# The norm between retention and the second MLP, with its multiplies divided among three engines

## The chip, the cores and the metric

The kernel runs on one core of one Trainium2 chip. The metric is device time in microseconds from the first to the last instruction with what lies around them; the time of a kernel is the median of several runs. The engines are named here as in the profile: PE is TensorE (PEld its weight loads), DVE is VectorE, ACT is ScalarE, POOL is GpSimd, SP issues DMAs.

## The reference

A decoder trunk of two layers works on 1024 positions of 1024 channels in float32. Layer 0 mixes by dilated attention and a short convolution, layer 1 by retention; after each mixer come an RMS norm and a gated MLP with a depthwise convolution of width 3. Only the last of these norms is touched:

```python
def rms_norm(x, g):
    xf = x.astype(jnp.float32)
    y = xf * lax.rsqrt(jnp.mean(xf * xf, axis=-1, keepdims=True) + EPS)
    return (y * g.astype(jnp.float32)).astype(x.dtype)

def conv_glu_ffn(xn, w_up, conv_w, w_down):
    u = causal_dwconv(xn @ w_up, conv_w)
    g, val = jnp.split(u, 2, axis=-1)
    return (jax.nn.silu(g) * val) @ w_down

        x = x + retention_mixer(...)
        x = x + conv_glu_ffn(rms_norm(x, ffn_norm[l]), ffn_w_up[l], ffn_conv_w[l], ffn_w_down[l])
```

## The kernel before

The residual stream stays on the chip as eight row tiles of 128 positions by 1024 channels (`xb`). Float32 products are made from a high and a low half of each operand: `split` (lines 107 to 110) casts the source on ScalarE (line 109, the high half) and subtracts it on GpSimd or VectorE (line 110, the low half); each product then takes three passes of TensorE (high by high, high by low, low by high).

The up-projections use one level of Strassen's scheme. Row tiles are taken in pairs, (0, 2), (1, 3), (4, 6) and (5, 7), one tile from each of the two row halves of the scheme's blocks. For each pair the class `Norming` (line 720) does four things, and a plan, a string of steps, says in which order the program writes them down:

- `q`: the sum of squares on ScalarE (line 163; its unused output goes to a scratch tile of the tag "s", of which there are three), then the inverse rms on GpSimd (lines 152 and 153);
- `r`: the normed rows. In the form that this norm has, VectorE multiplies each tile by the inverse rms and the norm weights in two instructions of 512 channels (`normed`, line 172);
- `t`: 16 transposes on TensorE (`turn`, line 179) into four PSUM banks of the tag "b", which has four;
- `c`: from the four transposed blocks, the seven operands of the scheme, split into halves (`xc`). `combine` (line 184) copies one block on ScalarE, makes four sums on VectorE (lines 196, 198, 199, 201) that all go to SBUF, and splits seven operands: three blocks straight from PSUM with their low halves on VectorE, the four sums with their low halves on GpSimd.

The class knows a second form, `spread=True`, which the norm ahead of the first MLP uses. A step `g` multiplies both tiles of the pair by the norm weights on GpSimd (`gain`, line 735), four instructions of 512 channels a pair. The step `r` then multiplies one tile by its inverse rms on ScalarE (line 764) and the other on VectorE (line 762), in place, in one instruction of 1024 channels each. And `c` is `combine_psum` (line 206): four sums again, but two of them are written over blocks in PSUM, so that VectorE makes five low halves and GpSimd two:

```python
        act.copy(b12, p12)
        put(0, p11)
        dve.tensor_tensor(t3, p22, b12, ALU.subtract)
        put(5, t3, pool)
        dve.tensor_tensor(t2, t3, p11, ALU.add)
        put(4, t2, pool)
        dve.tensor_tensor(p11, b12, p11, ALU.subtract)
        put(2, p22)
        put(1, p21)
        put(3, p11)
        dve.tensor_tensor(p21, t2, p21, ALU.subtract)
        put(6, p21)
```

Two other strands of work run through the plan. `d` is one step of the last output sweep of retention: 12 matmuls for one row tile (line 328) and two adds to `xb` (line 333). The sweep has eight steps, four for each of two groups of rows of the output weights, over the tiles 4, 6, 5, 7, so tiles 0 to 3 are complete before it starts and tiles 4 to 7 only near its end. `h` is one step of the first block of the up-projection (`first_block`, then `strassen`, line 231): one step that loads weights and forms sums of them (lines 274 to 276, scratch tiles of the tag "s" as well), then 14 products (line 245), seven on the columns of pairs 1 and 2 and seven on those of pairs 3 and 4. Each weight operand is split when its product is near; the low halves of the weight sums are instructions of VectorE (line 110, `hl<-s`).

Row tiles, the temporary tiles of `c`, the block's outputs and two of the four operands of the last sweep share five buffers of the tag "u". Before the plan starts, `play("q0 r0 q1")` (line 1357) is written down behind the last unit of retention. The plan is `PLAN_LATE` (line 35), played at line 1367. The program's order is not the exact order of an engine's queue: when the kernel is built, a planner lays each engine's instructions out by its own costs, and where several are ready takes the one written down first. On the chip each queue then runs in that fixed order.

Of the kernel before, what the change touches and what calls it, by code (L numbers as in the profile page):

```python
# [31 lines left out]
FILL = (1, 2)  # L32

PLAN = "s0 g0 q0 s1 q1 r0 t0 s2 q2 c0 g1 r1 s3 q3 t1 c1 g2 h1 r2 t2 h1 c2 g3 r3 h1 t3 h1 c3 h4"
PLAN_LATE = "d1 t0 d1 c0 r1 d1 t1 d1 c1 d2 q2 h1 r2 d1 t2 d1 q3 h1 c2 r3 h1 t3 h1 c3 h4"

PLAN_DOWN = (
    "a0 d2 a1 d2 a2 d2 a3 d2 A0 d3 b0 b1 B0 A1 B1",
# [36 lines left out]
def trunk(tc, a):  # L75
# [79 lines left out]
    def row_gains(g, parts):  # L155

        for i, t in enumerate(parts):
            sync.dma_start(out=t, in_=g[0:1, i * HALF : (i + 1) * HALF].to_broadcast([P, HALF]))
        return parts
# [178 lines left out]
    def run(gen):  # L338
        for _ in gen:
            pass  # L340
# [14 lines left out]
    g0 = row_gains(a["even_norm"][0:1], [np_.tile([P, HALF], f"g{i}") for i in range(2)])  # L355
    load_x(1)
    r0 = np_.tile([P, P], "r0")
# [295 lines left out]
    def fill(n):  # L653
        for _ in range(n):
            next(steps, None)
# [129 lines left out]
    nrm = Norming(a["ffn_norm"][0:1], spread=True)  # L785
# [377 lines left out]
    def fetch_q(h, half):  # L1163
        q = rt[0].tile([P, 2, 2, HALF], "q", 2, dt=F32R)
        sync.dma_start(out=f(q), in_=qscr[4 * h + 2 * half])
        return q

    def fetch_k(h, half):

        k, kf = rt[1].tile([P, 2, 2, HALF], "k", dt=F32R), None  # L1170
        sync.dma_start(out=f(k), in_=qscr[4 * h + 2 * half + 1])
        if half == 0:
            kf = rt[1].tile([P, 2, HALF], "kf")
            sync.dma_start(out=kf, in_=kscr[h])
        return k, kf
# [3 lines left out]
    def scores(q, k):  # L1179
        sT = rt[3].tile([P, 2, 1280], "sT", dt=F32R)  # L1180
        for j in range(4):
            n = HALF - j * P
            b = b_bank()
            for d in range(2):
                for i, (ks, qs) in enumerate(PASSES):
                    pe.matmul(
                        b[:, :n], k[:, ks, d, j * P : (j + 1) * P], q[:, qs, d, j * P :],
                        start=(d == 0 and i == 0), stop=(d == 1 and i == 2),
                    )
            t = wk.tile([P, HALF], "s", 3)  # L1190
            dve.tensor_tensor(t[:, :n], b[:, :n], unit0["tri"][:, :n], ALU.mult)
            split(sT[:, 0, SOFF[j] : SOFF[j] + n], sT[:, 1, SOFF[j] : SOFF[j] + n], t[:, :n], (pool, dve)[j % 2])
        return sT

    def key_rows(kf):

        kn = rt[3].tile([P, 4, HALF], "ky", dt=F32R).rearrange("p t (s d) -> p t s d", s=2)
        for t in range(4):
            pt = b_bank()
            for d in range(2):  # L1200
                pe.transpose(pt[:, d * P : (d + 1) * P], kf[:, d, t * P : (t + 1) * P], ident)
            act.copy(kn[:, t, 0, :], pt[:, :256])
            dve.tensor_tensor(kn[:, t, 1, :], pt[:, :256], f(kn[:, t, 0, :]), ALU.subtract)
        return kn

    def first_state(kn, v):

        pd = [o_bank(), o_bank()]
        for t in range(4):
            for d in range(2):  # L1210
                for i, (ks, vs) in enumerate(PASSES):
                    pe.matmul(
                        pd[d], kn[:, t, ks, d * P : (d + 1) * P], v[:, vs, t, :],
                        start=(t == 0 and i == 0), stop=(t == 3 and i == 2),
                    )
        st = rt[3].tile([P, 2, 2, HALF], "st", dt=F32R)
        for d in range(2):
            act.copy(st[:, 0, d, :], pd[d])
            dve.tensor_tensor(st[:, 1, d, :], pd[d], f(st[:, 0, d, :]), ALU.subtract)
        return st  # L1220

    def outputs(half, q, v, sT, st):
        y = f(rt[3].tile([P, 4, HALF], "ky", dt=F32R))
        held = []

        def scale(t, o, mv, r):
            dve.tensor_scalar(y[:, t, :], o, mv[:, 0:1], r, ALU.subtract, ALU.mult)

        for t in range(4):
            o = b_bank()  # L1230
            terms = [(sT[:, :, SOFF[j] + (t - j) * P : SOFF[j] + (t - j + 1) * P], v[:, :, j, :]) for j in range(t + 1)]
            if half:
                terms += [(q[:, :, d, t * P : (t + 1) * P], st[:, :, d, :]) for d in range(2)]
            for n, (l, r) in enumerate(terms):
                for i, (ls, rs) in enumerate(PASSES):
                    pe.matmul(
                        o, l[:, ls, :], r[:, rs, :], start=(n == 0 and i == 0), stop=(n == len(terms) - 1 and i == 2)
                    )
            bs, mv, r = rt[3].tile([P, 6], "bs", 3), rt[3].tile([P, 2], "mv", 3), sm.tile([P, 1], "rr", 8)
            dve.bn_stats(bs, o)  # L1240
            dve.bn_aggr(mv, bs)
            rsqrt_mean(r, mv[:, 1:2], 1, 1)
            held.append((t, o, mv, r))
            fill(OFILL[half][t])
            if t:
                scale(*held.pop(0))
        return y, lambda: scale(*held.pop(0))

    def gated(h, y, gt, last):
        if last:  # L1250
            t = h_tile()
            yT = [t[:, :, i * HALF : (i + 1) * HALF] for i in range(2)]
            yT += [u_tile().bitcast(F32R).rearrange("p (s t) -> p s t", s=2) for _ in range(2)]
        else:
            t = [yp.tile([P, 2, 2, HALF], f"y{i}", dt=F32R) for i in range(2)]
            yT = [t[c // 2][:, :, c % 2] for c in range(4)]
        for c in range(4):
            pt = b_bank()
            for t in range(4):
                pe.transpose(pt[:, t * P : (t + 1) * P], y[:, t, c * P : (c + 1) * P], ident)  # L1260
            dve.scalar_tensor_tensor(gt[:, c, :], pt, gncol(h, c), gt[:, c, :], ALU.mult, ALU.mult)
            split(yT[c][:, 0], yT[c][:, 1], gt[:, c, :], (pool, dve)[c % 2])
        return yT

    def wo_sweep(half, h, yT, g, tiles, after=None):
        def lhs(j):
            return lambda s, t: yT[2 * g + j][:, s, (t - 4 * half) * P : (t - 4 * half + 1) * P]

        return sweep(
            [lhs(j) for j in range(2)], [w_rows(wo, h * 4 + 2 * g + j) for j in range(2)], tiles, o_bank, after  # L1270
        )

    def fetch_v(h, half, queue=act):
        v = rt[4 if half else 2].tile([P, 2, 4, HALF], "v", dt=F32R)
        for s in range(2):
            queue.dma_start(out=f(v[:, s]), in_=vscr[2 * h + half, :, s])
        return v

    def fetch_g(h, half):
        t, ts = rt[3].tile([P, 4, HALF], "gt"), slice(half * HALF, (half + 1) * HALF)  # L1280
        sync.dma_start(out=t, in_=scr[4 * h : 4 * h + 4, :, ts].rearrange("a p t -> p a t"))
        return t
# [26 lines left out]
    for h in range(4):  # L1309
        for n, block in enumerate(blocks[h]):  # L1310
# [4 lines left out]
            c0 = (h * (4 if name == "ret_wg" else 2) + i) * P  # L1315
# [17 lines left out]
    for n, (h, half) in enumerate(units):  # L1333
        more = n + 1 < len(units)
        sT = scores(q, k)
        fill(SFILL[half][0])
        if half == 0:
            kn = key_rows(kf)
            fill(SFILL[half][1])
            st = first_state(kn, v)  # L1340
        if more:
            q2, (k, kf) = fetch_q(*units[n + 1]), fetch_k(*units[n + 1])
        y, finish = outputs(half, q, v, sT, st)
        if more:
            q = q2
            fill(SFILL[half][2])
            v = fetch_v(*units[n + 1])
        finish()
        if more:
            run(steps)  # L1350
        else:
            fill(2)
        yT = gated(h, y, gt, not more)
        if not more:
            run(steps)
            nrm = Norming(a["ffn_norm"][1:2])
            nrm.play("q0 r0 q1")
        if more:
            gt = fetch_g(*units[n + 1])
            tiles = range(4 * half, 4 * half + 4)  # L1360
            steps = chain(*[wo_sweep(half, h, yT, g, tiles) for g in range(2)])
# [4 lines left out]
    head = first_block(a["ffn_w_up"][1], 0, NFF * P, xc)  # L1366
    nrm.play(PLAN_LATE, xc, chain(*[wo_sweep(half, h, yT, g, ORDER[4:]) for g in range(2)]), head[0])

# [50 lines left out]
```

## Time and profile before

| | |
|---|---|
| three runs | 2714.38, 2716.61, 2719.99 us; median 2716.61 us |
| the profiled execution | 2716.35 us, of which its span 2714.6 us |
| granted TensorE clock, mean | 0.995 of full speed |
| HBM read, written | 257.38 MB, 77.07 MB |
| DMA, mean rate | 124 GB/s |

Every time in the views counts from the start of the span of the profiled execution. An engine is busy while an instruction of it runs; TensorE's matmuls overlap, so that a mean duration is longer than the distance from one to the next, and that distance is the better price. A name such as `u<-xb,rr,g` gives the tile written and the tiles read. The idle time in brackets is that of the engine just before the instruction, with the one that ended it.

### The profile page before, as it was taken

The page shows a single profiled execution, that of the slowest core. Times are in us where ns is not written, and L with a number is a line of the kernel's source. Part 1 is how long each engine was busy: PE and PEld are TensorE (multiplying, and loading weights), DVE is VectorE, ACT ScalarE, POOL GpSimd, SP SyncE. Part 2 cuts the span into 40 slices and gives each one's busy share as a digit, 9 for nine tenths or more (in the row PEclk, how much of TensorE's full clock was granted, in tenths as well). Part 3 has the DMA queues.
Part 4 walks back from the last instruction along what each step waited for, and adds up shares of the span by engine and source line. Part 5 has one row for each costly group of instructions (what it writes and reads, how often), then busy time and mean ns, then how long its engine had stood idle before and what let it go on. Part 6 is the DMA issues. An engine that isn't in the chain of part 4 may idle for free. (4 is left out here: it accounts for less than half of the span.)

```text
span 2714.6 us, 34985 instructions
## 1 busy us (share of the span) xinstructions
PE 2643.7 (97%) x12793; PEld 2167.6 (80%) x12793; DVE 1907.7 (70%) x2950; ACT 1189.6 (44%) x2050; POOL 795.3 (29%) x603
## 2 busy tenths in 40 slices
PE   8999999999999999989999999999999999999999
PEld 6877777778888888867979888788877888888887
DVE  4247776687777789697575665566578777777986
ACT  4345543454444444364444444222235444445444
POOL 6721113533343300033222122344454433331000
PEclk9999999999999999999999999999999999999999
DMA  5310012122222274424545556655421222225554
GB/s 173 104 47 28 24 36 78 40 75 90 74 85 79 78 271 151 159 84 143 187 163 167 185 166 244 243 191 194 155 70 56 82 82 78 85 71 194 201 185 143
DMA packets 258784, 336.74 MB, mean 124 GB/s; under 512 B 15120, under 2 KB 182196, under 8 KB 252468
## 3 DMA queue, kind: packets, MB, share of 16 engines
q1 hardware_dynamic: 224428, 246.94, 28.2%
q10 hardware_dynamic: 34184, 87.57, 8.8%
q8 instruction: 100, 1.64, 0.2%
q14 instruction: 72, 0.59, 0.1%
HBM read 257.38 MB, written 77.07 MB: 123 GB/s over the span
## 5 line engine op out<-in xcount | busy, mean ns | idle before, releaser
L110 POOL TENSOR_TENSOR hl<-raw,hl 128x512 fp32r<-128x512 f32 x347 | 580.4, 1687 | 1243.0 <-ACT hl L109 1121.5
L245 PE MATMUL b<-xc,hl 128*128 128x512 f32 (+1 forms) x2652 | 606.7, 389 | 4.7 <-POOL xc L110 3.0
L245 PE MATMUL o<-xc,hl 128*128 128x512 f32 (+1 forms) x2568 | 592.4, 391 | 14.1 <-ACT u L300 5.2
L245 PEld LDWEIGHTS b<-xc,hl 128*128 128x128 f32 x2652 | 488.1, 190 | 117.3 <-POOL xc L110 3.8
L245 PEld LDWEIGHTS o<-xc,hl 128*128 128x128 f32 x2568 | 474.9, 191 | 125.6 <-ACT u L300 7.6
L109 ACT CAST hl<-raw 128x512 fp32r<-128x512 f32 (+1 forms) x440 | 265.2, 609 | 515.0 <-PE o L328 136.8
L110 DVE TENSOR_TENSOR hl<-s,hl 128x512 fp32r<-128x512 f32 x309 | 219.3, 714 | 228.7 <-ACT hl L109 228.5
L972 DVE SCALAR_TENSOR_TENSOR u<-u,cc,u 128x1022 f32<-128x1022 f32 (+1 forms) x176 | 263.5, 1522 | 0.9
L109 ACT CAST hl<-s 128x512 fp32r<-128x512 f32 x309 | 189.8, 619 | 143.5 <-PE b L245 59.0
L458 PE MATMUL u<-xT,hl 128*128 128x512 f32 x576 | 166.1, 410 | 0.0
L328 PE MATMUL o<-hl,y 128*128 128x512 f32 x672 | 163.8, 398 | 0.0
L905 PE MATMUL o<-hl,hl 128*128 128x512 f32 x600 | 146.2, 395 | 5.6 <-DVE hl L110 3.5
L328 PEld LDWEIGHTS o<-hl,y 128*128 128x128 f32 x672 | 125.8, 189 | 29.3 <-DVE y L110 0.3
L905 PEld LDWEIGHTS o<-hl,hl 128*128 128x128 f32 x600 | 111.1, 188 | 35.0 <-DVE hl L110 7.4
L333 DVE TENSOR_TENSOR xb<-xb,o 128x512 f32<-128x512 f32 x160 | 105.1, 681 | 37.5 <-PE o L328 37.5
L458 PEld LDWEIGHTS u<-xT,hl 128*128 128x128 f32 x576 | 99.5, 189 | 20.6 <-issue 5.7
L970 ACT ACTIVATE u<-u,cc 128x1024 f32<-128x1024 f32 x88 | 100.9, 1151 | 31.3 <-DVE u L312 31.3
L109 ACT CAST hl<-h 128x512 fp32r<-128x512 f32 (+1 forms) x124 | 70.0, 581 | 84.9 <-PE b L905 23.2
L1063 PE MATMUL o<-hl,xc 128*128 128x256 f32 x768 | 95.8, 283 | 1.6 <-DVE u L315 1.6
L1063 PEld LDWEIGHTS o<-hl,xc 128*128 128x128 f32 x768 | 93.7, 188 | 2.8 <-DVE u L315 2.5
L110 DVE TENSOR_TENSOR hl<-h,hl 128x512 fp32r<-128x512 f32 (+1 forms) x124 | 77.6, 641 | 25.8 <-ACT hl L109 25.5
L152 POOL TENSOR_SCALAR rr<-ss 128x1 f32<-128x1 f32 (+1 forms) x48 | 14.5, 303 | 251.6 <-ACT s L163 233.4
(220 smaller groups left out, 4000.7 us busy)
## 6 DMA issues: line engine op xcount, KB each, us to landing
raw<-in_ffn_w_up SPq DMA_DIRECT2D x176, 256.0 KB, 3.0
raw<-in_ffn_w_down SPq DMA_DIRECT2D x176, 256.0 KB, 3.2
hs<-u ACTq DMA_DIRECT2D x44, 512.0 KB, 2.7
h<-hs SPq DMA_DIRECT2D x44, 512.0 KB, 6.1
raw<-in_even_w_in SPq DMA_DIRECT2D x73, 256.0 KB, 2.7
qscr<-h ACTq DMA_DIRECT2D x16, 1024.0 KB, 4.1
vscr<-u ACTq DMA_DIRECT2D x32, 512.0 KB, 4.1
raw<-in_ret_wo SPq DMA_DIRECT2D x64, 256.0 KB, 3.9
```

Source lines behind the costliest of these rows:

```text
L109: act.copy(hi, src)
L110: (eng or pool).tensor_tensor(lo, src, f(hi), ALU.subtract)
L152: pool.tensor_scalar(out, ss, 1.0 / n, EPS, ALU.mult, ALU.add)
L245: pe.matmul(u, hl[:, ws, k * P : (k + 1) * P], xc[b][:, xs, k, cols_], start=(first and k == 0 and i == 0), stop=(k == 3 and i == 2), skip ...
L328: pe.matmul(o, lhs[j](ls, t), ws[j][hf][:, w, :], start=(j == 0 and i == 0), stop=(j == n - 1 and i == 2),)
L333: dve.tensor_tensor(xs, xs, o, ALU.add)
L458: pe.matmul(u, hl(ws, k), xT[:, xs, k, hf * 512 : (hf + 1) * 512], start=(k == 0 and i == 0), stop=(k == KT - 1 and i == 2),)
L905: pe.matmul(o, l[:, ls, c * P : (c + 1) * P], r[:, ws, :], start=(start and i == 0), stop=(stop and i == 2), skip_group_check=True,)
L970: act.mul(c, u, wcol(2, jj))
L972: dve.scalar_tensor_tensor(c[:, d:], u[:, :-d], wcol(2 - d, jj), c[:, d:], ALU.mult, ALU.add)
L1063: pe.matmul(u[t // 2][:, c : c + 256], xc[b][:, xs, k, ts], hl[name][k // 2][:, ws, k % 2 * 256 : k % 2 * 256 + 256], start=(first and k = ...
```

## The change

The norm at the second MLP takes the second form. Step `g0` is written down ahead of the squares of the first pair, and three steps `g1`, `g2`, `g3` go into the plan: `g1` behind `c0`, `g2` ahead of `q2`, `g3` behind `c2`. The first two row tiles, the other steps and their order stay.

```diff
-PLAN_LATE = "d1 t0 d1 c0 r1 d1 t1 d1 c1 d2 q2 h1 r2 d1 t2 d1 q3 h1 c2 r3 h1 t3 h1 c3 h4"
+PLAN_LATE = "d1 t0 d1 c0 g1 r1 d1 t1 d1 c1 d2 g2 q2 h1 r2 d1 t2 d1 q3 h1 c2 g3 r3 h1 t3 h1 c3 h4"
...
-            nrm = Norming(a["ffn_norm"][1:2])
-            nrm.play("q0 r0 q1")
+            nrm = Norming(a["ffn_norm"][1:2], spread=True)
+            nrm.play("g0 q0 r0 q1")
```

By `spread=True` the multiplies of line 172 (16 instructions on VectorE) give way to those of lines 735 (16 on GpSimd), 762 (4 on VectorE) and 764 (4 on ScalarE), and `combine` gives way to `combine_psum`.

## The prediction

> **What bounds the kernel now.** I read the page first, for the share of each engine, then the busy time by stretches around the edited norm, then TensorE's instructions there in order of time, and last the chain of waits of the same stretch.
>
> ```profile
> span 2714.6 us, 34985 instructions
> PE 2643.7 (97%) x12793; PEld 2167.6 (80%) x12793; DVE 1907.7 (70%) x2950; ACT 1189.6 (44%) x2050; POOL 795.3 (29%) x603
> ```
>
> TensorE is busy for 97% of the span, so an edit that adds no matmul can win only where TensorE stands idle, or runs below its full clock. The edit touches one place, so that place is what I price.
>
> ```profile
> 2017.00:2046.20 29.20, 26.89 (x130) 21.11 (x128) 28.48 (x41) 17.95 (x34) 22.99 (x23) 1.00 0.16 46
> 2046.20:2080.60 34.40, 28.08 (x202) 25.57 (x203) 29.49 (x44) 18.03 (x37) 18.23 (x15) 0.95 0.19 54
> 2017.00:2080.60 63.60, 54.97 (x332) 46.68 (x331) 57.97 (x84) 35.98 (x70) 41.21 (x38) 0.97 0.18 50
> 2050.20:2066.40 16.20, 12.71 (x88) 11.83 (x88) 14.90 (x22) 8.39 (x17) 8.43 (x8) 0.89 0.11 33
> 2066.40:2080.60 14.20, 12.98 (x98) 12.01 (x99) 10.58 (x18) 8.39 (x18) 8.43 (x6) 1.00 0.20 56
> 497.50:565.70 68.20, 57.85 (x331) 50.31 (x330) 55.06 (x84) 39.32 (x73) 42.70 (x44) 0.92 0.17 49
> 532.20:565.70 33.50, 26.46 (x178) 24.53 (x179) 29.55 (x44) 18.18 (x36) 19.32 (x15) 0.90 0.23 68
> ```
>
> Each row gives a stretch, its length, and the busy time of TensorE, of its weight loads, of VectorE, ScalarE and GpSimd, then the granted clock. From the first matmul of the last output sweep (2017) to the first of the second up-projection block (2080.6) TensorE is idle for 63.60 - 54.97 = 8.6 us. In 2017 to 2046 the sweep covers nearly all (29.20 - 26.89 = 2.3 us idle). After it 34.40 - 28.08 = 6.3 us are idle. VectorE is the fullest other engine: 57.97 of 63.60 us, and 28.48 of the first 29.20. The last two rows are the norm ahead of the first MLP, which is already written the new way; I come back to them.
>
> ```profile
> 2046.58 0.63 PE L179 MATMUL b<-ident,u 128*128 128x128 f32 x4 [0.46 <-DVE u L172]
> 2047.82 1.09 PE L179 MATMUL b<-ident,u 128*128 128x128 f32 x8 [0.61 <-DVE u L172]
> 2049.49 0.66 PE L179 MATMUL b<-ident,u 128*128 128x128 f32 x4 [0.59 <-DVE u L172]
> 2056.62 0.50 PE L245 MATMUL o<-xc,hl 128*128 128x256 f32 x2 [0.32 <-ACT u L300]
> 2059.21 4.14 PE L245 MATMUL o<-xc,hl 128*128 128x256 f32 x20 [2.09 <-DVE hl L110]
> 2064.83 1.53 PE L179 MATMUL b<-ident,u 128*128 128x128 f32 x12 [1.04 <-DVE u L172]
> 2069.09 2.52 PE L245 MATMUL b<-xc,hl 128*128 128x256 f32 x14 [0.34 <-DVE xc L110]
> 2072.27 7.13 PE L245 MATMUL b<-xc,hl 128*128 128x256 f32 x57 [0.66 <-POOL xc L110]
> ```
>
> Brackets hold the idle time ahead and who ended it. The transposes of the third pair of row tiles wait for their normed rows (0.46 + 0.61 + 0.59 = 1.66 us), a Strassen product waits 2.09 us for its weights' low halves, the transposes of the fourth pair wait 1.04 us for rows, and the second half of the block waits for the last operands (0.34 and 0.66). After the 2.09 us, 20 matmuls take 4.14 us, or 0.207 each, where 57 later ones take 7.13, or 0.125: 20 x 0.082 = 1.6 us more, in the stretch whose granted clock is 0.89. So about 6.3 + 1.6 = 8 us can be won after the sweep, and 2.3 before it.
>
> ```profile
> 2040.62 1.87 DVE xb L333 x3
> ...
> 2045.77 1.50 DVE u L172 x3
> 2047.68 1.75 DVE u L172
> 2049.44 2.39 DVE xb L333 x4
> 2051.83 1.21 DVE hl L110 x2
> 2057.78 1.39 DVE hl L110
> 2059.53 1.16 ACT s L163 x2
> 2064.70 0.74 DVE u L172
> ```
>
> In the chain of waits of this stretch VectorE works through four row multiplies (2045.77 and 2047.68, 3.25 us), four residual adds, and two low halves, then the sums of the third pair, and only then (2057.78) the low half that TensorE waits for. The squares of the fourth pair (2059.53) hang on the same instruction: their scratch tile is one of three that the weight sums hold. So one late VectorE queue sets both waits.
>
> **The change, part by part.** These rows are from the stretch itself (old form) and from the first norm (new form).
>
> ```profile
> L172 DVE SCALAR_TENSOR_TENSOR u<-xb,rr,g 128x512 f32<-128x512 f32 x16 | 15.8, 1025 | 1.9 <-POOL rr L153 1.9
> L110 POOL TENSOR_TENSOR xc<-u,xc 128x512 fp32r<-128x512 f32 x16 | 21.9, 1404 | 15.2 <-DVE u L199 15.2
> L110 DVE TENSOR_TENSOR xc<-b,xc 128x512 fp32r<-128x512 f32 x12 | 8.2, 684 | 0.1
> L735 POOL TENSOR_TENSOR u<-xb,g 128x512 f32<-128x512 f32 x16 | 20.7, 1320 | 6.4 <-DVE xb L333 4.4 <-PE b L179 2.0
> L762 DVE TENSOR_SCALAR u<-u,rr 128x1024 f32<-128x1024 f32 x4 | 4.7, 1174 | 4.7 <-POOL rr L153 3.6 <-POOL u L735 1.1
> L764 ACT ACTIVATE u<-u,rr 128x1024 f32<-128x1024 f32 x4 | 4.6, 1152 | 4.3 <-POOL rr L153 3.2 <-POOL u L735 1.1
> ```
>
> *VectorE* loses the 16 row multiplies (15.8 us) and gains 4 multiplies by the inverse rms (4.7) and 8 low halves that GpSimd did (8 x 0.684 = 5.5): net -5.6 us over four pairs. The four Strassen sums a pair stay on it. *ScalarE* gains 4 x 1.152 = 4.6 us; it works 36 of 63.6 us now, so there is room, though each 1.15 us stands in its queue ahead of casts. *GpSimd* gains 16 gains (20.7) and loses 8 low halves (8 x 1.404 = 11.2): net +9.5 us on 41.21, still under the span. No DMA moves or is added.
>
> ```profile
> 2027.46 2.70 DVE L172 SCALAR_TENSOR_TENSOR u<-xb,rr,g 128x512 f32<-128x512 f32 x2
> 2030.68 2.85 DVE L172 SCALAR_TENSOR_TENSOR u<-xb,rr,g 128x512 f32<-128x512 f32 x2
> ```
>
> ```profile
> L153 POOL TENSOR_TENSOR rr<-rr,mhalf 128x1 f32<-128x1 f32 x8 | 5.8, 726 | 0.7
> L152 POOL TENSOR_SCALAR rr<-ss 128x1 f32<-128x1 f32 x8 | 3.8, 480 | 4.3 <-ACT s L163 3.8
> ```
>
> The first two rows are the old multiplies of pair 2 in order of time, the other two GpSimd's inverse rms, 0.73 + 0.48 = 1.2 us a tile.
>
> *Pairs 1 and 2 (under the sweep).* The two gains of pair 2 (4 x 1.32 = 5.3 us) and two low halves (2.8) now stand in one GpSimd queue ahead of its rows, where VectorE needed 2.70 + 2.85 us for the row multiplies. I take zero; bounds -2.3 us (all idle under the sweep goes) and +2 (rows later by a low half and a half gain). Two Strassen sums stay in PSUM, so their banks come free with the last low half instead of one step earlier; the next transposes come later than that by rows alone, so nothing.
>
> *Pair 3.* Its gains can start when the adds under the sweep are done; four take 5.3 us, then comes the inverse rms. Its adds are the last in the chain (2040.62, 1.87 us), so the first gain can start at about 2041.3 and the second row stands at 2041.3 + 5.3 + 1.2 (inverse rms) + 1.2 (multiply) = 2049.0, against 2049.4 now. I take zero; bounds -1.66 (all of that idle goes) and +2.5 (one more tile's gain ahead).
>
> *The low halves of the weight sums.* VectorE saves 3.25 - 1.17 = 2.1 us ahead of them, and its four adds (2.39) may go while GpSimd multiplies. That opens some 2 to 4 us before the sums of pair 3 can start, as these wait for transposes. Two low halves of 0.7 to 1.5 us fit, as two do already at 2051.83. I take it that they go there: the waits of 0.32 and 2.09 and the slow clock after them vanish, -4.0 us. At worst they stay behind nine instead of seven VectorE operations of pair 3 and gain 2.1 - 1.4 = 0.7 us.
>
> *Pair 4.* Its squares start with that same release, so the 1.04 us ahead of its transposes go too: -1.0; at worst 0, if gains are late. Its sums now end with two GpSimd low halves instead of four, so I take off half of the last 0.34 + 0.66: -0.5; bounds -1.0 and +1.0 (nine VectorE operations instead of seven).
>
> Sum: -4.0 - 1.0 - 0.5 = -5.5 us. The profiled execution took 2716.35 us, its span 2714.6 plus 1.75 around it; 2716.35 - 5.5 = 2710.8. The median of the three runs is 0.26 above that execution, so I say **2711.0 us**.
>
> **A rule against it.** GpSimd and VectorE slow each other here:
>
> ```profile
> L172 DVE SCALAR_TENSOR_TENSOR u<-xb,rr,g x16: 739/752/1764, 2016.7 to 2064.7; 128x512 f32<-128x512 f32 x16
> L762 DVE TENSOR_SCALAR u<-u,rr x4: 752/1100/1742, 509.0 to 545.8; 128x1024 f32<-128x1024 f32 x4
> ```
>
> The same instruction (least, median, most ns) takes 739 or 1764. If each of the net 9.5 us that GpSimd gains held VectorE up, its -5.6 would become +3.9 us, and that is a rival below. The trace so far speaks half for it: the median of the old multiply is 752, so most are not held. [...]
>
> **The rivals.**
>
> *The form gives here what it gave ahead of the first MLP.* From the third pair's first transpose to the second block that norm took 33.50 us, with no squares waiting for scratch, against 34.40 here. Taken as it is, the edit wins 0.9 us; with the low halves staying behind pair 3 about 2 to 3. That gives 2714 to 2716, say **2714.7**: no measurable change.
>
> *GpSimd becomes the queue that ends last, and the kernel slows.*
>
> ```profile
> 528.45 5.48 POOL L735 TENSOR_TENSOR u<-xb,g 128x512 f32<-128x512 f32 x4
> 533.88 2.94 POOL L110 TENSOR_TENSOR xc<-u,xc 128x512 fp32r<-128x512 f32 x2
> PE o L245 <- POOL xc L110: 3.0, 1, 3.0
> ```
>
> In the first norm four gains stood ahead of two low halves, and TensorE waited 3.0 us. The whole stretch there is 68.20 us for the same matmuls, 4.6 more than here. If the third or fourth pair meets that queue, with VectorE held up by the 3.9 us worked out above, the time is 2716.6 + 4.6 = **2721**. It decides once the third pair's second row comes more than 5.5 us after 2049.4. Against it: there the first block had begun before the second pair's operands were done, while here these are finished under the sweep, and operands of pairs 3 and 4 are first needed by the second half of the block, seven products later.
>
> *More goes.* If the idle time under the sweep (2.3) and half of the third pair's 1.66 go as well, the sum is -8.6: **2708**.
>
> **How the numbers follow.** Forecast case (2709 to 2713): 0.40. Same as in the first norm (2713 to 2717): 0.30. More goes (2706 to 2709): 0.15. Slower (2717 to 2723): 0.15. About 0.2%, or 5.4 us, is what a measurement of this kernel can tell from no change, so the line lies at 2711.2, through the middle of the forecast case: faster 0.40 x 0.6 + 0.15 = 0.39, slower (above 2722) 0.07, within 0.54. The range runs from **2707.0** (2.3 and all of 1.66 would reach 2706.9) to **2718.0**, which takes in every part at nothing (2716.6) and the first quarter of the slower case; it leaves out the rest of that case and a little of the larger gain.
>
> **What would show it.** Right: the 2.09 us wait ahead of the weight-sum product is gone and the granted clock stays near 1.00 between 2050 and 2066; the squares of pair 4 start five or more us earlier against the end of pair 3's transposes; the distance from the first matmul of the last sweep to the second block is about 58 us instead of 63.6; VectorE is busy about 52 us there and GpSimd about 50. Wrong: the low halves of the weight sums still stand behind pair 3's sums; a TensorE wait of over 2 us released by GpSimd's gains, by the multiply on ScalarE, or by GpSimd's inverse rms; or the row operations on VectorE all near their longest.

## The result, and the profile after

The changed kernel is slower. Its median is 2725.43 us (2723.15 to 2730.73, seven runs) beside 2718.8 us (2714.38 to 2719.99, seven runs, the first three among them) of the kernel before. The medians differ by 6.6 us and the means by 8.5. The ratio that is used from here on is taken from all fourteen runs: 1.0032, with a 95% interval of 1.0023 to 1.0041, about 8.7 us more (6.3 to 11.1). The forecast was 2711.0 us in a range of 2707 to 2718.

The profiled execution took 2727.95 us. First two lines of its page, then the busy time by stretches (the columns are those of the rows in the prediction): from the last sweep's first matmul to the third pair's first transpose, from there to the second block, and both together.

```profile
span 2726.2 us, 34974 instructions
PE 2648.3 (97%) x12793; PEld 2170.9 (80%) x12793; DVE 1901.2 (70%) x2946; ACT 1194.3 (44%) x2054; POOL 801.1 (29%) x611
```

```profile
2020.40:2058.10 37.70, 29.96 (x128) 23.16 (x126) 26.30 (x38) 22.06 (x38) 29.24 (x28) 0.91 0.12 35
2058.10:2091.60 33.50, 26.37 (x205) 25.20 (x205) 27.72 (x44) 20.43 (x40) 18.37 (x18) 0.95 0.21 60
2020.40:2091.60 71.20, 56.34 (x333) 48.37 (x331) 54.03 (x81) 42.49 (x76) 47.61 (x45) 0.93 0.16 47
```

The whole stretch takes 71.2 us where it took 63.6. All of that, and a little more, lies in its first part, under the sweep: 37.7 us against 29.5. The row of the kernel before, up to the third pair's first transpose as well:

```profile
2017.00:2046.50 29.50, 26.89 (x130) 21.11 (x128) 28.78 (x42) 18.25 (x35) 22.99 (x23) 1.00 0.16 45
```

In that part TensorE is idle for 37.70 - 29.96 = 7.7 us (2.6 before), and busy 29.96 - 26.89 = 3.1 us longer for two matmuls fewer, at a granted clock of 0.91 instead of 1.00. From the third pair on it takes 33.5 us where it took 34.1. Over the whole stretch the work of the engines came out near the forecast, and leaves room: VectorE has 54.0 us of it (58.0 before), GpSimd 47.6 (41.2 before). But GpSimd's work is not spread evenly. Until pair 2's second row is done, before (first two rows) and after (last two), the stretches are:

```profile
2017.00:2023.00 6.00, 5.42 (x33) 4.52 (x32) 5.28 (x8) 4.26 (x9) 5.50 (x9) 1.00 0.32 90
2023.00:2035.00 12.00, 10.35 (x52) 7.94 (x51) 12.00 (x16) 6.21 (x12) 9.98 (x7) 1.00 0.20 59
```

```profile
2020.40:2025.80 5.40, 3.52 (x15) 2.28 (x14) 0.69 (x1) 4.40 (x7) 5.23 (x6) 1.00 0.00 0
2025.80:2041.40 15.60, 11.50 (x52) 9.06 (x50) 10.10 (x15) 8.93 (x17) 14.65 (x15) 0.87 0.24 68
```

GpSimd, the last engine of each row, is busy there for 5.50 + 9.98 = 15.5 of 18.0 us before, and for 5.23 + 14.65 = 19.9 of 21.0 us after. So in this part it is nearly full, which the sum over the whole stretch hides, and what stands late in its queue comes late.

TensorE in order of time, in the changed kernel:

```profile
2023.11 0.50 PE L328 MATMUL o<-hl,h 128*128 128x512 f32 x1 [0.37 <-ACT hl L109]
2025.12 0.73 PE L328 MATMUL o<-hl,h 128*128 128x512 f32 x2 [1.51 <-POOL hl L110]
2026.91 2.52 PE L179 MATMUL b<-ident,u 128*128 128x128 f32 x12 [0.62 <-DVE u L762]
...
2041.49 1.94 PE L179 MATMUL b<-ident,u 128*128 128x128 f32 x8 [3.36 <-DVE u L762]
...
2058.17 0.66 PE L179 MATMUL b<-ident,u 128*128 128x128 f32 x4 [1.74 <-ACT u L764]
...
2070.86 4.08 PE L245 MATMUL o<-xc,hl 128*128 128x256 f32 x20 [4.24 <-DVE hl L110]
2076.62 2.04 PE L179 MATMUL b<-ident,u 128*128 128x128 f32 x16 [1.68 <-ACT u L764]
...
2081.33 8.61 PE L245 MATMUL b<-xc,hl 128*128 128x256 f32 x72
```

The same places in the kernel before, the sweep's first step and pair 2's late transposes:

```profile
2017.10 2.94 PE L328 MATMUL o<-hl,h 128*128 128x512 f32 x12
...
2031.91 1.09 PE L179 MATMUL b<-ident,u 128*128 128x128 f32 x8 [1.03 <-DVE u L172]
2033.59 0.66 PE L179 MATMUL b<-ident,u 128*128 128x128 f32 x4 [0.58 <-DVE u L172]
```

The sweep's very first step waits for its weights' halves (0.37 and 1.51 us; there was no such wait before), pair 2's transposes wait 3.36 us for a row (1.03 and 0.58 before), and the product on the weight sums waits 4.24 us (2.09 before). Only the last line is a gain: the second half of the block runs without the two waits of 0.34 and 0.66 us that it had.

GpSimd in order of time over the same part, and VectorE's two multiplies that the late rows need:

```profile
2018.37 5.48 POOL L735 TENSOR_TENSOR u<-xb,g 128x512 f32<-128x512 f32 x4
2023.81 1.26 POOL L110 TENSOR_TENSOR hl<-raw,hl 128x512 fp32r<-128x512 f32 x1
...
2028.32 3.77 POOL L110 TENSOR_TENSOR hl<-raw,hl 128x512 fp32r<-128x512 f32 x3
2032.05 2.56 POOL L735 TENSOR_TENSOR u<-xb,g 128x512 f32<-128x512 f32 x2
2034.57 1.28 POOL L110 TENSOR_TENSOR xc<-u,xc 128x512 fp32r<-128x512 f32 x1
2035.82 1.27 POOL L735 TENSOR_TENSOR u<-xb,g 128x512 f32<-128x512 f32 x1
2037.06 1.28 POOL L110 TENSOR_TENSOR xc<-u,xc 128x512 fp32r<-128x512 f32 x1
2038.32 1.25 POOL L735 TENSOR_TENSOR u<-xb,g 128x512 f32<-128x512 f32 x1
```

```profile
2039.61 1.74 DVE L762 TENSOR_SCALAR u<-u,rr 128x1024 f32<-128x1024 f32 x1 [1.50 <-POOL u L735]
2059.52 0.75 DVE L762 TENSOR_SCALAR u<-u,rr 128x1024 f32<-128x1024 f32 x1 [0.72 <-POOL rr L153]
```

The four gains of pair 1 (5.48 us) run ahead of the low halves of the sweep's weights, and the first of these (2023.81) is the one that TensorE waits 1.51 us for; in the kernel before, two of them ran from 2015.88, ahead of the sweep. Three more (2028.32) then stand ahead of pair 2's gains, which alternate with the low halves of pair 1's sums until 2039.6. Pair 2's second row is done at 2041.4. The third pair's second row comes at 2060.3, 39.8 us after the sweep's start, where the old one came at 2049.44, 32.3 us after it.

### The profile page after: what moved, and what is told of

It reads as the page before. It is cut to its first block, busy times and chain, and to the rows that moved or that the text cites. A ratio compares the mean times of both kernels' runs of the same rounds, so it can differ in the third digit from the quotient of the medians.

```text
span 2726.2 us, 34974 instructions
## 1 busy us (share of the span) xinstructions
PE 2648.3 (97%) x12793; PEld 2170.9 (80%) x12793; DVE 1901.2 (70%) x2946; ACT 1194.3 (44%) x2054; POOL 801.1 (29%) x611
```

## The experiments

The sweep's first matmul falls between 2013.5 and 2023.2 us in the profiled executions of these kernels, although almost nothing ahead of it differs. So beside the ratio of the timed runs, the stretch from that matmul to the second block is given, as a difference of starts in one profiled execution each. Four kernels whose timed runs cannot be told apart (before, e2, e4 and e10) lie within 0.5 us of each other in it. Some of these kernels have one line more, so that L763 and L765 are lines 762 and 764 there.

| kernel | sweep starts | third pair's transposes | second block | stretch, us | ratio to before, 95% interval |
|---|---|---|---|---|---|
| before | 2017.10 | 2046.58 | 2080.65 | 63.55 | |
| changed | 2020.48 | 2058.17 | 2091.54 | 71.06 | 1.0032 (1.0023 to 1.0041) |
| e1, new rows, old sums | 2018.33 | 2056.38 | 2093.77 | 75.44 | 1.0044 (1.0031 to 1.0056) |
| e2, old rows, new sums | 2018.34 | 2047.73 | 2082.21 | 63.87 | 0.9999 (0.9990 to 1.0007) |
| e3, new rows in pairs 1, 2 | 2014.99 | 2051.65 | 2086.03 | 71.04 | 1.0030 (1.0018 to 1.0042) |
| e4, new rows in pairs 3, 4 | 2023.18 | 2053.47 | 2086.66 | 63.48 | 1.0007 (0.9998 to 1.0016) |
| e5, pair 1 old | 2017.53 | 2050.32 | 2086.36 | 68.83 | 1.0020 (1.0011 to 1.0028) |
| e6, pair 2 old | 2014.99 | 2048.61 | 2081.85 | 66.86 | 1.0009 (1.0000 to 1.0018) |
| e7, pair 2's transposes later | 2015.94 | 2049.30 | 2088.05 | 72.11 | 1.0048 (1.0034 to 1.0061) |
| e9, e2 with weight sums' low halves on GpSimd | 2013.51 | 2042.88 | 2074.47 | 60.96 | 0.9988 (0.9979 to 0.9997) |
| e10, before with the same edit | 2016.88 | 2046.38 | 2080.29 | 63.41 | 0.9997 (0.9988 to 1.0006) |
| e11, changed, sweep's low halves on VectorE | 2014.88 | 2049.06 | 2086.05 | 71.17 | 1.0021 (1.0012 to 1.0030) |

**Rows alone.** The class got a separate switch for the sums:

```diff
-            nrm = Norming(a["ffn_norm"][1:2], spread=True)
+            nrm = Norming(a["ffn_norm"][1:2], spread=True, psum=False)
```

> The row multiplies in the new form for all four pairs (GpSimd by the norm weights, ScalarE and VectorE by the inverse rms), the Strassen sums in the old form (all in SBUF, four low halves a pair on GpSimd). Theory Q (GpSimd's queue under the sweep): the loss sits between the first matmul of the last sweep and the third pair's first transpose, 37.7 us in the changed kernel against 29.5 before, because gains stand in GpSimd's queue ahead of the sweep weights' low halves and of pair 2's rows, and sweep steps stand behind pair 2's transposes in TensorE's fixed order. Then this kernel is slower than before by 6 to 11 us (GpSimd has even 11 us more to do than in the changed kernel). Rival P (the sums in PSUM are the cost: nine VectorE operations a pair instead of seven, banks held longer): within 2 us of before. Rival L (GpSimd and VectorE hold each other up in every pair alike): slower by 6 to 9 us, the longest VectorE operations spread over all four pairs.

Slower than before by 0.44%, about 12 us (8.4 to 15.2), a little over what theory Q gave. Its stretch is 11.9 us longer: 8.6 us of that under the sweep, as Q says, and 3.3 behind it, which Q did not name. Rival P falls; the total alone does not decide against rival L. The new rows carry the loss. By the stretches the new sums take 4.4 us of it back, though the timed intervals of this kernel and the changed one overlap.

VectorE here makes the low halves of the weight sums ahead of the third pair's sums:

```profile
2062.39 5.18 DVE L110 TENSOR_TENSOR hl<-s,hl 128x512 fp32r<-128x512 f32 x3
2067.49 0.68 DVE L196 TENSOR_TENSOR u<-u,b 128x512 f32<-128x512 f32 x1
```

So they went where the prediction had put them, and TensorE does not wait for them. But they take 5.18 us, where 1.88 us are enough in the next kernel, beside 5.15 us of gains on GpSimd (from 2063.58), and the fourth pair's transposes then wait 4.07 us for a row.

**Sums alone.** The plan and rows of before, `combine_psum` for all pairs:

```diff
-            nrm = Norming(a["ffn_norm"][1:2])
+            nrm = Norming(a["ffn_norm"][1:2], psum=True)
```

> The row multiplies in the old form on VectorE for all pairs, the plan of before, the Strassen sums in the new form with two of them in PSUM. Theory Q: within 3 us of before, either way, with the 29.5 us of the stretch under the sweep changed by less than 2. Rival P: slower by 6 to 9 us. Rival L: GpSimd has 11 us less to do, so VectorE's row multiplies come nearer to their shortest (739 ns) and the kernel is faster by 2 to 5 us.

No change that can be measured (2.7 us faster to 1.9 slower); the part under the sweep takes 29.4 us, as before. Rival P, which wanted 6 us or more, falls; rival L, which wanted a gain of 2 to 5 us, finds none. But where the time goes within the block changed. VectorE and TensorE of this kernel:

```profile
2053.51 0.68 DVE L110 TENSOR_TENSOR xc<-b,xc 128x512 fp32r<-128x512 f32 x1
...
2058.62 0.68 DVE L110 TENSOR_TENSOR xc<-b,xc 128x512 fp32r<-128x512 f32 x1
2059.22 1.88 DVE L110 TENSOR_TENSOR hl<-s,hl 128x512 fp32r<-128x512 f32 x3
```

```profile
2047.73 0.63 PE L179 MATMUL b<-ident,u 128*128 128x128 f32 x4 [0.34 <-DVE u L172]
...
2059.95 2.24 PE L245 MATMUL o<-xc,hl 128*128 128x256 f32 x13 [3.75 <-DVE hl L110]
```

All three low halves of the weight sums (2059.22) come after the nine operations of the third pair's sums (2053.51 to 2058.62 and its end), and TensorE waits 3.75 us, 1.7 longer than before. The last waits are 0.6 us shorter than before (one of 0.37 us in place of 0.34 and 0.66).

**New rows in two pairs at a time.** `r` takes the old form for the pairs named, and their `g` steps are left out of the plan; the sums are new for all pairs.

```diff
-                        if not self.spread:
+                        if not self.spread or n in self.old:
```

> As the changed kernel, but only pairs 1 and 2 have their rows in the new form; pairs 3 and 4 have the old row multiplies on VectorE. Sums in PSUM for all. Theory Q: all of the loss stays, slower than before by 6 to 10 us, and the stretch under the sweep takes about 37 us. Rival L: half of it, 3 to 5 us. Rival P: 6 to 9 us here and in the next kernel alike.

> As the changed kernel, but only pairs 3 and 4 have their rows in the new form; pairs 1 and 2 have the old row multiplies on VectorE. Sums in PSUM for all. Theory Q: the loss is gone, between 4 us faster and 1 us slower than before, and the stretch under the sweep takes 29 to 31 us. Rival L: slower by 3 to 5 us. Rival P: slower by 6 to 9 us.

With new rows in pairs 1 and 2 the stretch is 71.04 us, the same as in the changed kernel; with new rows in pairs 3 and 4 it is 63.48, the same as before. The part under the sweep takes 36.7 and 30.3 us, as theory Q has it. In time e3 is 8.2 us slower than before (4.9 to 11.4), in Q's range. e4 is 1.9 us slower (0.5 faster to 4.3 slower), which lies between Q's range and rival L's and decides nothing by itself. The stretches decide: rival L wanted half of the loss in each kernel, rival P all of it in each.

**One pair old.** The same switch, for pair 1 or for pair 2 alone.

> As the changed kernel, but pair 1 keeps the old row multiplies on VectorE; pairs 2, 3 and 4 have the new form. It splits the 7.5 us by which the stretch from the last sweep's first matmul to the second block grew (63.55 to 71.06 us). Theory Q1 (two separate queues): the waits of the sweep's first step for its weights (0.37 on ScalarE's casts and 1.51 on GpSimd's low halves, behind the four gains of pair 1) are gone, with some slow clock, and the 3.4 us ahead of pair 2's transposes stay: slower than before by 3 to 6 us. Rival Q2 (all of it follows from the late first step): within 2 us of before. Rival Q3 (pair 2 alone is the cause): slower than before by 6 to 9 us.

> As the changed kernel, but pair 2 keeps the old row multiplies on VectorE; pairs 1, 3 and 4 have the new form. Theory Q1: the 3.4 us ahead of pair 2's transposes are gone, the waits of the sweep's first step stay: slower than before by 2 to 4 us. Rival Q2: slower by 6 to 9 us. Rival Q3: within 2 us of before.

TensorE of the first and of the second of them:

```profile
2035.21 1.06 PE L179 MATMUL b<-ident,u 128*128 128x128 f32 x8 [3.80 <-DVE u L763]
```

```profile
2019.62 1.01 PE L328 MATMUL o<-hl,h 128*128 128x512 f32 x2 [1.51 <-POOL hl L110]
2020.42 3.43 PE L179 MATMUL b<-ident,u 128*128 128x128 f32 x16
...
2033.19 1.50 PE L179 MATMUL b<-ident,u 128*128 128x128 f32 x12 [0.55 <-DVE u L172]
```

With pair 1 old the sweep's first step no longer waits, and pair 2's wait stays, at 3.80 us: the stretch is 2.2 us shorter than in the changed kernel. With pair 2 old the 1.51 us stay, and pair 2 waits 0.55: 4.2 us shorter. Both old (e4) give 7.6. So the two waits are separate, and account for 6.4 of 7.5 us; the rest goes only when both go. In time the two kernels are 5.4 us (3.0 to 7.6) and 2.4 us (0.0 to 4.9) slower than before, in Q1's ranges. Q2 falls by these times. Q3 is not ruled out by the times, but by the stretches, which are 5.3 and 3.3 us over the one before where it wants all and nothing, and by the 1.51 us that stay with pair 2 old.

**Pair 2's transposes later.** All work is the same; two sweep steps go ahead of `t1`.

```diff
-PLAN_LATE = "... c0 g1 r1 d1 t1 d1 c1 d2 g2 ..."
+PLAN_LATE = "... c0 g1 r1 d3 t1 c1 d1 g2 ..."
```

> The changed kernel with one step moved: pair 2's transposes are written down two sweep steps later, and come after the first group of the sweep and one step of the second in TensorE's order. All work is the same. Theory Q1 holds that rows that come late cost TensorE time only because sweep steps stand behind the transposes in its fixed order: the 3.4 us wait is covered, and the kernel is 2 to 5 us faster than the changed kernel, so slower than before by 3 to 6 us. Rival (the rows' own lateness passes on through pair 2's sums and VectorE's adds to pair 3): as slow as the changed kernel, 7 to 10 us over before.

A miss: it is no faster than the changed kernel. It is 13 us slower than before (9.2 to 16.6), more than the rival gave too; its stretch, taken in the fastest of its five runs, accounts for 8.6 us of that, and the rest is not explained. TensorE and VectorE here:

```profile
2037.56 2.92 PE L328 MATMUL o<-hl,u 128*128 128x512 f32 x7 [4.33 <-DVE xb L333]
```

```profile
2035.08 1.74 DVE L762 TENSOR_SCALAR u<-u,rr 128x1024 f32<-128x1024 f32 x1 [1.50 <-POOL u L735]
2036.74 0.67 DVE L333 TENSOR_TENSOR xb<-xb,o 128x512 f32<-128x512 f32 x1
```

The sweep now waits 4.33 us for an add on VectorE to free its PSUM bank, and that add stands in VectorE's order behind the multiply that waits for GpSimd's gain. The late row reaches the sweep by a second road. So the fixed order of VectorE, not that of TensorE alone, lets it through, and the sweep does not cover it. The rival is nearer the mark than theory Q1, in that the lateness passes on through VectorE's adds, though here to the sweep and not to pair 3.

**GpSimd relieved, gains kept.** The low halves of the last sweep's weights go to VectorE:

```diff
-    nrm.play(PLAN_LATE, xc, chain(*[wo_sweep(half, h, yT, g, ORDER[4:]) for g in range(2)]), head[0])
+    nrm.play(PLAN_LATE, xc, chain(*[wo_sweep(half, h, yT, g, ORDER[4:], eng=dve) for g in range(2)]), head[0])
```

> The changed kernel with one edit: the low halves of the eight weight blocks of the last sweep are made on VectorE, not on GpSimd (8 x about 0.7 us more there, 8 x 1.3 us less on GpSimd). The gains and everything else stay. Theory Q1 (GpSimd's queue: gains ahead of the sweep weights' low halves, and these ahead of pair 2's gains): the sweep's first step has no wait on GpSimd, pair 2's second row comes 3 us or more earlier, and the kernel is 3 to 6 us faster than the changed kernel, so 2 to 6 us slower than before. Rival (VectorE and GpSimd hold each other up, or the gains are too long by themselves): no faster than the changed kernel, 7 to 10 us slower than before.

Two views of TensorE, in order of time and by stretches:

```profile
2018.85 0.73 PE L328 MATMUL o<-hl,h 128*128 128x512 f32 x2 [0.84 <-DVE hl L110]
...
2032.73 1.33 PE L179 MATMUL b<-ident,u 128*128 128x128 f32 x8 [1.95 <-DVE u L762]
```

```profile
2014.80:2049.00 34.20, 28.59 (x128) 21.84 (x126) 29.68 (x43) 21.80 (x38) 24.16 (x23) 0.95 0.14 39
2049.00:2086.10 37.10, 30.58 (x205) 29.59 (x205) 27.41 (x44) 20.83 (x40) 18.42 (x18) 0.82 0.19 57
```

Both waits shrink (1.51 to 0.84, 3.36 to 1.95) and the part under the sweep is 3.5 us shorter than in the changed kernel, which is what the theory asks; pair 2's second row comes 3.2 us earlier, counted from the sweep's start. In the profiled execution all of it is lost again behind, where TensorE is busy 30.58 us for matmuls that took 26.37, at a clock of 0.82; what lowers the clock there is not shown. The timed runs put the kernel at 1.0021, some 3 us better than the changed one, but the intervals overlap (1.0012 to 1.0030, 1.0023 to 1.0041). I count it as support for GpSimd's queue under the sweep, and as inconclusive for the total.

**A version that is faster than both.** e2, with the low halves of the three weight sums of this block on GpSimd; and the kernel before with that edit alone:

```diff
-        subs = {11: pool, 12: pool, 22: pool} if np_ == 1 else {}
+        subs = {11: pool, 12: pool, 22: pool} if np_ == 1 else low or {}
...
-    head = first_block(a["ffn_w_up"][1], 0, NFF * P, xc)
+    head = first_block(a["ffn_w_up"][1], 0, NFF * P, xc, 0, {"s1": pool, "s2": pool, "s3": pool})
```

> The kernel with the old row multiplies and two sums in PSUM (the second experiment), with one more edit: in this block the low halves of the three weight sums are made on GpSimd, not on VectorE. Where the sums are in PSUM, TensorE waits 3.75 us for such a low half behind pair 3's nine VectorE operations. If that queue is the cause, the wait and the slow clock behind it go, and the squares of pair 4 start sooner: faster than before by 2 to 6 us. Rival (GpSimd's own low halves, 1.3 us each and held up by VectorE, come as late): within 2 us of before.

> The kernel before with one edit: in the first block of the second up-projection the low halves of the three weight sums are made on GpSimd, not on VectorE. It shows what the edit of the kernel that beat both is worth without the sums in PSUM. If GpSimd's queue is what decides, its four low halves of pair 3 (old form) stand beside the three of the weight sums, and the gain is smaller than with two sums in PSUM: within 2 us of before, the stretch from the sweep to the second block 62 to 64 us. Rival (VectorE's queue alone decides): as fast as with the sums in PSUM, 2 to 5 us faster than before, the stretch 60 to 61.5 us.

With the new sums it is faster than before: 0.9988 (0.9979 to 0.9997), about 3.3 us (0.8 to 5.7), the stretch 60.96 us. Without them no change can be measured, and the rival of e10 falls. GpSimd and TensorE of the faster one, then VectorE of the kernel before and of e10, and TensorE of e10:

```profile
2042.45 4.76 POOL L110 TENSOR_TENSOR hl<-s,hl 128x512 fp32r<-128x512 f32 x3
```

```profile
2046.24 2.79 PE L179 MATMUL b<-ident,u 128*128 128x128 f32 x12 [2.73 <-DVE u L172]
2048.68 8.89 PE L245 MATMUL o<-xc,hl 128*128 128x256 f32 x71
```

```profile
2045.70 3.74 DVE L172 SCALAR_TENSOR_TENSOR u<-xb,rr,g 128x512 f32<-128x512 f32 x4
```

```profile
2045.49 5.77 DVE L172 SCALAR_TENSOR_TENSOR u<-xb,rr,g 128x512 f32<-128x512 f32 x4
```

```profile
2049.64 1.09 PE L179 MATMUL b<-ident,u 128*128 128x128 f32 x8 [2.63 <-DVE u L172]
...
2064.75 1.53 PE L179 MATMUL b<-ident,u 128*128 128x128 f32 x12 [1.21 <-DVE u L172]
...
2071.93 7.12 PE L245 MATMUL b<-xc,hl 128*128 128x256 f32 x57 [0.66 <-POOL xc L110]
```

In the faster one 71 matmuls of the block's first half run without a stop, and the wait of 3.75 us is gone. Part of it is paid back: beside GpSimd's low halves VectorE's multiplies of the third pair take longer (in e10 5.77 us for four, against 3.74 in the kernel before by the same view), and the transposes wait 2.6 to 2.7 us. e10 pays this too, keeps the last wait for GpSimd (0.66), and comes out even. That these waits are the reason is read from the views; no run tests it.

## Why the prediction was wrong

*The step that failed first: "Pairs 1 and 2 (under the sweep) ... I take zero; bounds -2.3 us and +2".* It measured +7.6 us: e4, which keeps those two pairs' old rows, has a stretch of 63.48 us, and the changed kernel 71.06. By the prediction's own figures the queue ahead of pair 2's rows grew from 5.55 to 8.1 us, and I held that the sweep covers it. But the sweep needs GpSimd too, for its weights' low halves. I left these out: the four gains of pair 1 went ahead of the first of them (e5: 2.2 us), and three more, 3.77 us, stood ahead of pair 2's gains. "Still under the span" was a sum over 63.6 us; in the part that counts GpSimd went from 15.5 of 18.0 us to 19.9 of 21.0. And pair 2's late row stopped the sweep itself, by TensorE's order in the changed kernel and by VectorE's adds in e7 (e6: 4.2 us).

*"The low halves of the weight sums ... I take it that they go there": -4.0 us.* It did not come. The wait grew from 2.09 to 4.24 us, and e2 shows that the new sums do it without the new rows (3.75): their operations came one behind another with no gap, and the low halves stood behind all of them. With the new rows and the old sums (e1) they went ahead and the wait was gone, so it is the new sums that keep them behind, and this step gave them no weight. But in e1 the low halves were slow, and a wait of 4.07 us came behind them. The "at worst", a gain of 0.7, was too kind as well. With the new sums, the old rows and these low halves on GpSimd (e9) the kernel is 3.3 us faster than before.

*"Pair 3 ... I take zero".* Near enough by itself. Its adds end at 2053.4 in the changed kernel and its second row at 2060.3, 6.9 us later; before it was 2042.5 and 2049.4, 6.9 us too. The row was late because the sweep was. The waits at its transposes grew, from 1.66 to 1.74 + 1.13 = 2.9 us, and e4 shows that this costs the stretch nothing.

*"Pair 4 ... -1.0; ... -0.5".* The first half is wrong: its transposes wait 1.68 us, not 1.04, since its squares still hang on the weight sums' low halves. The second is right: the 0.34 and 0.66 us are gone.

*The sums of work.* They were near: VectorE 52 forecast and 54.0 measured, GpSimd 50 and 47.6. Taken over the whole stretch, they decided nothing.

*The rule against it.* It assumed that each of the net 9.5 us that GpSimd gains holds VectorE up; by it VectorE was to end 3.9 us over what it had, and it has 3.9 us less work. Single instructions of the changed kernel agree with a hold: the multiply by the inverse rms takes 0.75 us at 2059.52, where GpSimd is idle, and 1.74 where a GpSimd operation began just before (2039.54 in the trace, 2039.61 for VectorE). As a sum the measurement decides: VectorE's work fell by 3.9 us where 5.6 were forecast, and the 1.7 us between are far from the 9.5 that the rule asked for.

*The rival that slowed.* Its mechanism, GpSimd as the queue that ends last, is the one that came, with a chance of 0.15 and a price of 4.6 us; measured 8.7. Its deciding point, the third pair's second row over 5.5 us later, was met (7.5 us, counted from the sweep's start). Its place was wrong: I put it at pairs 3 and 4, where e3 and the changed kernel, 71.04 and 71.06 us, show that the new rows cost nothing, and argued that pairs 1 and 2 were safe under the sweep.

*Slips that change nothing.* 2716.35 - 5.5 + 0.26 is 2711.1. Spread evenly over 2717 to 2723, the part of the slower case above 2722 has a chance of 0.025 and not 0.07, and the range takes in a sixth of that case and not a quarter. The row of 29.20 us ends 0.4 us ahead of the third pair's first transpose, so 2.6 us were idle under the sweep and not 2.3.

What stays open: how much of pair 2's 4.2 us is the queue's length and how much VectorE being held up by GpSimd. The multiply of 1.74 us, where others take 0.75, is one such case and worth about 1 us. In e11 it takes 0.75, but GpSimd's queue is shorter there as well, so no kernel here took the one away without the other. Every edit also lets the planner lay out all queues anew: e2, e4, e6 and e9 share a wait of 1.2 to 1.3 us in the sweep, for an add on VectorE, that neither the kernel before nor the changed one has.

## What to carry to other kernels

A stretch in which TensorE is covered by other matmuls is covered only as long as those matmuls' own helpers are free: list what each engine's queue holds for the cover before giving that engine more. The busy sums of engines over a long stretch say nothing of this; here VectorE was relieved by 3.9 us, GpSimd was busy for 47.6 of 71.2 us, and the kernel lost 8.7, since GpSimd was busy for 19.9 of the 21 us in which the late rows were made. Take such sums over the part in which the moved work has to be done. Ask of each moved instruction which late result stands behind it, and move the one low half that the next product waits for before moving the bulk.

## What the runs showed of the hardware

Under the sweep of the changed kernel the granted clock fell to 0.50 after waits of 0.37, 1.51 and 0.62 us, and the longer busy time at the lower clock (3.1 us) is more than half of the added idle time (5.1 us). The changed kernel's first two stops, by stretches (its first row holds the waits, the second what follows):

```profile
2023.00:2026.00 3.00, 1.38 (x6) 0.93 (x7) 0.00 (x0) 3.00 (x6) 2.81 (x4) 1.00 0.00 0
...
2028.00:2030.00 2.00, 2.00 (x9) 1.90 (x8) 0.47 (x1) 1.33 (x3) 2.00 (x3) 0.50 0.00 0
```

TensorE was busy for 1.38 of 3 us, in pieces, and from two microseconds later ran at a granted clock of 0.50. From 2009.8 us until then no single wait was longer than 1.51 us. In the kernel before, 3.31 busy of 5 us (2046 to 2051) left the clock at 1.00, there and in the next 3 us. What lowers the clock after the one and not after the other is not shown. Of the 8.2 us by which the part under the sweep grew, 5.1 are added idle time, and 3.1 are longer busy time at the lower clock (0.91 instead of 1.00).
